# Projection banks of two token blocks, and a PSUM tile for scores alone

## Chip, cores and metric

The kernel runs on one core of a Trainium2 chip. The metric is device time of one execution in microseconds (us); the time before is the median of three runs. Four compute engines work from queues of their own, each in order: TensorE (PE, matmuls), VectorE (DVE), ScalarE (ACT) and GpSimd (POOL); SP issues the loads. Matmuls write to PSUM, which has eight banks of 512 fp32 values per partition; a bank goes to a new owner when its last reader has ended.

## What is computed

Two layers of an encoder on 512 tokens of width 1024, all fp32 in and out. Cut to what matters here:

```
h = rmsnorm(x, g_attn)
qa, ka, va, qb, kb, vb = split(h @ w_in)      # widths 512 128 128 512 512 512
qa, ka, qb, kb = rope(rmsnorm per head of 64) # each with a gain of its own
ya = windowed attention(qa, ka, va, sink)     # 8 query heads, 2 key heads, +/-128 tokens
yb = softmax(q1 k1) v - lam * softmax(q2 k2) v, normalised per head   # 4 heads
x = x + concat(ya, yb) @ w_out
h = rmsnorm(x, g_ffn); gate, val = split(h @ w_up)       # 2816 each
x = x + (silu(conv3(gate)) * val) @ w_down
```

## The kernel before

Activations stand transposed (features on partitions) as eight tiles of 128 x 512. To keep fp32 accuracy every operand is split into a high part and a low rest, and `mm3` makes each product of three matmuls. Weights come in units (`emit_unit`): one load, a cast on ACT (L193), a subtraction on DVE or POOL (L194).

`project` multiplies the four token blocks of 128 tokens by a chunk of 256 columns of `w_in`: 24 matmuls of 256 columns per block into one PSUM bank (half of it used), then a callback takes the bank. For queries and keys that is `qk_out`: ACT reads the bank and applies the row norm (`raw`, L343), ACT squares, DVE sums per head (`ss`) and scales (`sv`), POOL takes a power (`rs`, `rqa` or `rqb`, L255); for keys DVE multiplies by `rs` (L354); then rope: a product with the swapped halves (L360), a product with the cosine table (L364) and a sum (L365), the last two on POOL; then PE transposes the block into the single `tq` bank (`tr_qa`, `tr_bk` and so on, L369), and ACT and DVE split it into high and low (L258, L259). Values (`bv_done`) go from the bank through one instruction of ACT and one of DVE (L375, L376).

Attention runs as a generator, `attend`: first 8 steps of windowed attention (`a_scores`, `a_values`), then 16 of differential attention (`b_scores`, `b_weights`, `b_values`, `b_norm`). `a_scores` makes two score tiles of two banks (`sc_a`), whose masked maxima DVE takes (L429); ACT makes exponentials, DVE normalises the rows (`so_a`, L454), PE transposes them (`pt_a`, L470). `b_scores` makes one score tile of two banks (`sc_b`): a maximum on DVE (L518), a small product (L519), two exponentials on ACT (`e_b`, L522), a reciprocal (L526), the combination (L530); `b_weights` transposes it (`wt_b`, L542), `b_values` multiplies by values (`yb`), `b_norm` sums squares (`ss_yb`) and spreads factors over partitions (`rt_yb`).

`weave` writes these steps alternately with those of the projections and of the output projection (`wo`). A scheduler then orders each engine's instructions with a cost model of its own, and gives out buffers of pools by tag. What stands where in an engine's queue is thus fixed before the run. PSUM's tags: `mm` two banks, `at` two tiles of two banks (scores, some transposes, early projections), `acc` one, `tq` one. The channel mixer takes banks by `wide2`, in turn two `at` tiles and the pair of `mm`. SBUF: `rp` holds `raw` and the squares (7 tiles of one block), `tab` the rope tables (3), `sum` one norm sum.

Of the kernel before, what the change touches and what calls it, by code (L numbers as in the profile page):

```python
# [33 lines left out]
RP = 7  # L34
# [8 lines left out]
def kernel(  # L43
# [38 lines left out]
    def rp(name):  # L82
        return sb.tile([P, CW], F32, tag="rp", bufs=RP, name=name)

# [9 lines left out]
    def at2(name):  # L94
        return ps.tile([P, 2, S], F32, tag="at", bufs=2, name=name)
# [9 lines left out]
    def wide2(name):  # L105
        cyc["i"] += 1
        if cyc["i"] % 3 == 0:
            return mm(f"{name}a"), mm(f"{name}b")
        t = at2(name)
        return t[:, 0], t[:, 1]  # L110

    def halves(pick):
        have = []

        def alloc(name):
            if not have:
                have.extend(pick(name))
            return have.pop(0)
        return alloc

    def both(name):
        t = at2(name)
        return t[:, 0], t[:, 1]
# [130 lines left out]
    def rsqrt(o, i):  # L254
        nc.gpsimd.tensor_tensor(out=o, in0=i, in1=nhalf.broadcast_to([P, i.shape[1]]), op=ALU.pow)  # L255
# [23 lines left out]
    for l in range(depth):  # L279
# [43 lines left out]
        def project(name, done, alloc):  # L323
            w = [next_unit(), next_unit()]
            for t in range(NT):
                bank = alloc(f"pj{l}_{name}_{t}")
                for k in range(NK):
                    mm3(bank[:, :CW],
                        (h_in.hi[k][:, t * P:(t + 1) * P], h_in.lo[k][:, t * P:(t + 1) * P]),
                        (w[k // 4][0][:, k % 4, :], w[k // 4][1][:, k % 4, :]), k == 0, k == NK - 1)  # L330
                    if k % 4 == 3:
                        if k == NK - 1:
                            done(bank, t)
                        yield 1.3

        def qk_out(bank, t, n, tab, dst, nm, rq):
            nh = n // HD
            nm = f"{nm}{l}_{t}"
            if n == P:
                raw = bank  # L340
            else:
                raw = rp(f"raw_{nm}")
                nc.scalar.activation(raw, bank[:, :n], AF.Copy, scale=r_tok[:, t:t + 1])  # L343
            sq = rp(f"sq_{nm}")[:, :n]
            nc.scalar.activation(sq, raw, AF.Square)
            ss = smp(f"ss_{nm}", nh)
            nc.vector.tensor_reduce(out=ss, in_=sq.rearrange("p (h d) -> p h d", d=HD), axis=AX, op=ALU.add)
            sv = smp(f"sv_{nm}", nh)
            rv = raw.rearrange("p (h d) -> p h d", d=HD)
            if rq is None:  # L350
                nc.vector.tensor_scalar(out=sv, in0=ss, scalar1=1.0 / HD, scalar2=EPS, op0=ALU.mult, op1=ALU.add)
                rs = smp(f"rs_{nm}", nh)
                rsqrt(rs, sv)
                nc.vector.tensor_tensor(out=rv, in0=rv, in1=rs.unsqueeze(2).broadcast_to([P, nh, HD]), op=ALU.mult)  # L354
            else:
                nc.vector.tensor_scalar(out=sv, in0=ss, scalar1=EPS * HD, scalar2=None, op0=ALU.add)
                rsqrt(rq, sv)
            tb = sq
            sv_ = tab[:, 1, t].rearrange("p (two d) -> p two d", two=2).unsqueeze(1).broadcast_to([P, nh, 2, 32])
            (nc.vector if nm[1] == "a" else nc.gpsimd).tensor_tensor(out=tb.rearrange("p (h two d) -> p h two d", two=2, d=32),  # L360
                                    in0=raw.rearrange("p (h two d) -> p h two d", two=2, d=32)[:, :, ::-1, :],
                                    in1=sv_, op=ALU.mult)
            cv = tab[:, 0, t].unsqueeze(1).broadcast_to([P, nh, HD])
            nc.gpsimd.tensor_tensor(out=rv, in0=rv, in1=cv, op=ALU.mult)  # L364
            nc.gpsimd.tensor_tensor(out=raw, in0=raw, in1=tb, op=ALU.add)  # L365
            tr = tq(f"tr_{nm}")
            nb = n // P
            for b in range(nb):
                nc.tensor.transpose(tr[:, b * P:(b + 1) * P], raw[:, b * P:(b + 1) * P], ident)  # L369
            split_out(dst[0][:, :, t * P:(t + 1) * P] if nb > 1 else dst[0][:, t * P:(t + 1) * P],  # L370
                      dst[1][:, :, t * P:(t + 1) * P] if nb > 1 else dst[1][:, t * P:(t + 1) * P],
                      tr[:, :n].rearrange("p (b q) -> p b q", q=P) if nb > 1 else tr[:, :n])
# [11 lines left out]
        def akv_done(bank, t):  # L384
            raw = rp(f"raw_kv{l}_{t}")
            nc.scalar.activation(raw, bank[:, :CW], AF.Copy, scale=r_tok[:, t:t + 1])
            split_out(va[0][:, t * P:(t + 1) * P], va[1][:, t * P:(t + 1) * P], raw[:, P:])
            qk_out(raw[:, :P], t, P, tabs[1], ka, "ka", None)

        run(project("akv", akv_done, halves(both)))  # L390
# [4 lines left out]
        def proj_a(i, alloc):  # L395
            yield from project(f"aq{i}", lambda bank, t: qk_out(
# [94 lines left out]
        def bv_done(half, bank, t):  # L491
            if t % 2 == 0:
                v = keep(f"vb{l}_{half}_{t}")
                vb[half, t // 2] = (v[:, 0], v[:, 1])
# [316 lines left out]
```

## Time and profile before

| | |
|---|---|
| runs | 1347.71, 1350.54, 1353.40 us; median 1350.54 |
| profiled execution | 1350.17 us, span on the core 1348.4 us |
| busy: PE, DVE, ACT, POOL | 1256.2, 759.9, 550.7, 382.9 us |
| loads | 102.93 MB, 76 GB/s over the span |

The profiled execution is a run of its own. Its span goes from the first to the last instruction; the 1.8 us around it belong to the execution's time. "Idle before" and waits are put down to what ended them. PEclk is the clock granted to PE as a share of full speed: 0.50 is half. In rows of tiles the three numbers are shortest, median and longest duration in ns; in the timeline they are start and duration in us.

### The profile page before, as it was taken

What the parts mean: (1) busy time and instruction counts of PE and PEld (TensorE: products, weight loads), DVE (VectorE), ACT (ScalarE), POOL (GpSimd) and SP (SyncE); (2) the same over time, 40 slices, a digit from 0 to 9 for tenths busy, and PEclk for the clock granted to TensorE, in tenths of its full rate; (3) what the DMA queues carried; (4) which work ended last, traced back from release to release, by engine and by line L of the source; (5) the groups of instructions that cost most, each with busy time, mean ns of one, the idle gap of its engine ahead of it and who ended that gap; (6) DMA issues with size and microseconds to landing.
All of it is one profiled execution on the core that took longest, in us unless ns stands there. A gap on an engine that the chain in (4) does not pass through costs nothing.

```text
span 1348.4 us, 17285 instructions
## 1 busy us (share of the span) xinstructions
PE 1256.2 (93%) x6648; PEld 1048.1 (78%) x6648; DVE 759.9 (56%) x1345; ACT 550.7 (41%) x1003; POOL 382.9 (28%) x438
## 2 busy tenths in 40 slices
PE   6988799899999999999999688989999999999998
PEld 5977687687888778887788576967888887788876
DVE  6657687667555324554357676757755543355432
ACT  4445565445433212333345455634544331233321
POOL 5855377123211000110147461742221110011100
PEclk7998899699999999999999989989999999999999
DMA  4211122012332233332322020111133222333232
GB/s 167 82 44 32 40 63 63 16 47 79 95 101 90 82 101 94 98 100 69 98 91 63 32 63 8 57 63 32 48 99 104 94 87 90 106 94 97 83 102 78
DMA packets 32625, 102.93 MB, mean 76 GB/s; under 512 B 3616, under 2 KB 4000, under 8 KB 32544
## 3 DMA queue, kind: packets, MB, share of 16 engines
q1 hardware_dynamic: 32544, 101.84, 24.3%
q8 instruction: 52, 0.85, 0.3%
q14 instruction: 29, 0.24, 0.1%
HBM read 99.73 MB, written 2.10 MB: 76 GB/s over the span
## 4 chain that ended last, share of the span: by engine, by line
PE 75%; DVE 12%; ACT 5%; issue 4%; POOL 3%; DMA 1%; SPq 0%; POOLq 0%; ACTq 0%; DVEq 0%
PE up L207 8%; PE up L208 8%; PE up L206 8%; PE dn L207 4%; PE dn L206 4%; PE dn L208 4%; ACT so_a L447 2%; DVE so_a L454 2%; PE wo L206 1%; PE wo L207 1%; PE wo L208 1%; PE sc_b L516 1%; DVE so_a L429 1%; ACT wh L193 1%; PE wt_b L542 1%
## 5 line engine op out<-in xcount | busy, mean ns | idle before, releaser
L193 ACT CAST wh<-wr 128x1024 fp32r<-128x1024 f32 (+3 forms) x210 | 197.6, 945 | 401.4 <-PE up L207 151.7
L194 DVE TENSOR_TENSOR wl<-wr,wh 128x1024 fp32r<-128x1024 f32 (+3 forms) x174 | 191.7, 1105 | 170.0 <-ACT wh L193 165.0
L716 POOL TENSOR_TENSOR cv<-cv,rb 128x512 f32<-128x512 f32 x44 | 57.0, 1297 | 536.5 <-ACT cv L715 536.5
L207 PE MATMUL up<-nf_l,wh 128*128 128x512 f32 x464 | 180.9, 390 | 1.0 <-DVE nf_l L225 1.0
L206 PE MATMUL up<-nf_h,wh 128*128 128x512 f32 x464 | 180.6, 389 | 0.0
L208 PE MATMUL up<-nf_h,wl 128*128 128x512 f32 x464 | 180.5, 389 | 0.0
L194 POOL TENSOR_TENSOR wl<-wr,wh 128x1024 fp32r<-128x1024 f32 x36 | 86.7, 2413 | 99.4 <-ACT wh L193 85.7
L207 PEld LDWEIGHTS up<-nf_l,wh 128*128 128x128 f32 x464 | 87.1, 188 | 19.7 <-DVE nf_l L225 1.9
L206 PE MATMUL dn<-act,wh 128*128 128x512 f32 x240 | 96.1, 400 | 6.4 <-ACT wh L193 3.5
L206 PEld LDWEIGHTS up<-nf_h,wh 128*128 128x128 f32 x464 | 87.1, 188 | 18.1
L208 PEld LDWEIGHTS up<-nf_h,wl 128*128 128x128 f32 x464 | 87.1, 188 | 17.8
L207 PE MATMUL dn<-act,wh 128*128 128x512 f32 x240 | 95.9, 400 | 0.4 <-DVE act L259 0.4
L208 PE MATMUL dn<-act,wl 128*128 128x512 f32 x240 | 94.9, 398 | 0.0
L522 ACT ACTIVATE e_b<-sc_b,mx_b,rqb 128x512 f32<-128x512 f32 x64 | 49.3, 775 | 49.0 <-DVE mx_b L519 42.2
L709 DVE TENSOR_TENSOR gp<-up,rb 128x512 f32<-128x512 f32 x29 | 20.1, 692 | 80.6 <-PE up L208 79.6
L206 PEld LDWEIGHTS dn<-act,wh 128*128 128x128 f32 x240 | 45.4, 189 | 20.9 <-ACT wh L193 4.3
L715 ACT ACTIVATE cv<-cv 128x512 f32<-128x512 f32 x44 | 27.6, 632 | 79.7 <-DVE cv L714 79.6
L207 PEld LDWEIGHTS dn<-act,wh 128*128 128x128 f32 x240 | 45.8, 191 | 11.9 <-DVE act L259 1.1
L208 PEld LDWEIGHTS dn<-act,wl 128*128 128x128 f32 x240 | 45.4, 189 | 10.6
L206 PE MATMUL pj_bv<-wh,na_h 128*128 128x256 f32 x128 | 41.0, 320 | 7.7 <-DVE vb L376 7.7
L731 DVE TENSOR_TENSOR x<-x,dn 128x512 f32<-128x512 f32 x22 | 15.1, 688 | 52.8 <-PE dn L208 52.8
L470 PE MATMUL pt_a<-ident,so_a 128*128 128x128 f32 x160 | 28.3, 293 | 17.3 <-DVE so_a L454 12.0
(506 smaller groups left out, 3268.6 us busy)
## 6 DMA issues: line engine op xcount, KB each, us to landing
wr<-w_up SPq DMA_DIRECT2D x88, 512.0 KB, 3.6
wr<-w_in SPq DMA_DIRECT2D x36, 512.0 KB, 3.5
wr<-w_down SPq DMA_DIRECT2D x32, 384.0 KB, 3.1
wr<-w_down SPq DMA_DIRECT2D x32, 320.0 KB, 2.9
wr<-w_out SPq DMA_DIRECT2D x16, 512.0 KB, 3.7
x<-xT SPq DMA_DIRECT2D x8, 256.0 KB, 5.7
outT<-x SPq DMA_DIRECT2D x8, 256.0 KB, 2.0
rows<-row_par SPq DMA_DIRECT2D x2, 260.0 KB, 4.2
```

Of the source, the lines that this page charges most:

```text
L193: nc.scalar.copy(hi[:, o], raw[:, o])
L194: eng.tensor_tensor(out=lo[:, o], in0=raw[:, o], in1=hi[:, o], op=ALU.subtract)
L206: nc.tensor.matmul(acc, lhsT=a[0], rhs=b[0], start=start, stop=False)
L207: nc.tensor.matmul(acc, lhsT=a[0], rhs=b[1], start=False, stop=False)
L208: nc.tensor.matmul(acc, lhsT=a[1], rhs=b[0], start=False, stop=stop)
L447: nc.scalar.activation(so[i][:, :n], so[i][:, :n], AF.Exp, bias=ngm[:, i:i + 1], scale=rqa[:, qb, 2 * ip + i // 2, i % 2:i % 2 + 1], accum ...
L454: nc.vector.tensor_scalar(out=so[i][:, :n], in0=so[i][:, :n], scalar1=rl[:, i:i + 1], scalar2=None, op0=ALU.mult)
L470: nc.tensor.transpose(tr[:, o:o + P], so[2 * i + g][:, b * P:(b + 1) * P], ident)
L522: nc.scalar.activation(e[c], sc[c], AF.Exp, bias=mx[:, c:c + 1], scale=rq[:, c:c + 1], accum_out=lsum[:, c:c + 1])
L709: nc.vector.tensor_tensor(out=g[:, 1:S + 1], in0=acc[0], in1=rb, op=ALU.mult)
L715: nc.scalar.activation(cv, cv, AF.Silu)
L716: nc.gpsimd.tensor_tensor(out=cv, in0=cv, in1=rb, op=ALU.mult)
```

## The change

PSUM: a tag `sc` with one tile of two banks is for scores; `at` becomes two single banks, for transposes. A projection bank takes two token blocks side by side, and one callback handles both: ACT reads them one by one (the row norm differs), everything behind it works on both at once, and all transposes of the pair share the `tq` bank. The key's scaling by `rs` moves behind rope. All of windowed attention's transposes go to `at`. `wide` deals five banks in turn (two `mm`, two `at`, one half of `sc`). `rp` becomes four tiles of two blocks; the norm sum shares the ring of the tables.

```diff
-RP = 7
+RP = 4
     def rp(name):
-        return sb.tile([P, CW], F32, tag="rp", bufs=RP, name=name)
+        return sb.tile([P, 2, CW], F32, tag="rp", bufs=RP, name=name)
-    def at2(name):
-        return ps.tile([P, 2, S], F32, tag="at", bufs=2, name=name)
+    def at(name):
+        return ps.tile([P, S], F32, tag="at", bufs=2, name=name)
+
+    def sc2(name):
+        return ps.tile([P, 2, S], F32, tag="sc", bufs=1, name=name)
...
+    def wide(name):
+        cyc["i"] += 1
+        i = cyc["i"] % 5
+        return sc2(name)[:, 0] if i == 4 else (mm, at)[i % 2](name)
+
+    def turn(name):
+        cyc["i"] += 1
+        return (mm, at)[cyc["i"] % 2](name)
...
-            self.part = [sb.tile([P, S], F32, tag="sum", bufs=1, name=f"{name}_sum")]
+            self.part = [sb.tile([P, S], F32, tag="tab", bufs=3, name=f"{name}_sum")]
...
         def project(name, done, alloc):
             w = [next_unit(), next_unit()]
-            for t in range(NT):
-                bank = alloc(f"pj{l}_{name}_{t}")
...
+            for tp in range(NT // 2):
+                bank = alloc(f"pj{l}_{name}_{tp}").rearrange("p (t c) -> p t c", t=2)
+                for i in range(2):
+                    t = 2 * tp + i
+                    for k in range(NK):
+                        mm3(bank[:, i], (h_in.hi[k][:, t * P:(t + 1) * P], h_in.lo[k][:, t * P:(t + 1) * P]),
+                            (w[k // 4][0][:, k % 4, :], w[k // 4][1][:, k % 4, :]), k == 0, k == NK - 1)
+                        if k % 4 == 3:
+                            if i and k == NK - 1:
+                                done(bank, tp)
+                            yield 1.3
+
+        def scaled(name, bank, tp):
+            raw = rp(name)
+            for i in range(2):
+                nc.scalar.activation(raw[:, i], bank[:, i], AF.Copy, scale=r_tok[:, 2 * tp + i:2 * tp + i + 1])
+            return raw
+
+        def qk_out(raw, tp, tab, dst, nm, rq):
...
+            ss = smp(f"ss_{nm}", 2 * nh).rearrange("p (t h) -> p t h", t=2)
+            nc.vector.tensor_reduce(out=ss, in_=heads(sq), axis=AX, op=ALU.add)
...
-                nc.vector.tensor_tensor(out=rv, in0=rv, in1=rs.unsqueeze(2).broadcast_to([P, nh, HD]), op=ALU.mult)
...
+            for i in range(2):
+                sv_ = tab[:, 1, 2 * tp + i].rearrange("p (two d) -> p two d", two=2).unsqueeze(1).broadcast_to([P, nh, 2, 32])
+                (nc.vector if nm[1] == "a" else nc.gpsimd).tensor_tensor(
+                    out=tb[:, i].rearrange("p (h two d) -> p h two d", two=2, d=32),
+                    in0=raw[:, i].rearrange("p (h two d) -> p h two d", two=2, d=32)[:, :, ::-1, :],
+                    in1=sv_, op=ALU.mult)
+            cv = tab[:, 0, t2].unsqueeze(2).broadcast_to([P, 2, nh, HD])
+            nc.gpsimd.tensor_tensor(out=heads(raw), in0=heads(raw), in1=cv, op=ALU.mult)
             nc.gpsimd.tensor_tensor(out=raw, in0=raw, in1=tb, op=ALU.add)
-            tr = tq(f"tr_{nm}")
+            if rq is None:
+                nc.vector.tensor_tensor(out=heads(raw), in0=heads(raw), in1=rs.unsqueeze(3).broadcast_to([P, 2, nh, HD]),
+                                        op=ALU.mult)
             nb = n // P
+            tr = tq(f"tr_{nm}")[:, :nb * CW].rearrange("p (b q) -> p b q", b=nb)
             for b in range(nb):
-                nc.tensor.transpose(tr[:, b * P:(b + 1) * P], raw[:, b * P:(b + 1) * P], ident)
...
+                for i in range(2):
+                    nc.tensor.transpose(tr[:, b, i * P:(i + 1) * P], raw[:, i, b * P:(b + 1) * P], ident)
+            o = slice(tp * CW, (tp + 1) * CW)
+            split_out(dst[0][:, :, o], dst[1][:, :, o], tr)
...
-        run(project("akv", akv_done, halves(both)))
...
+        run(project("akv", akv_done, turn))
...
             for i in range(2):
-                sc = both(f"sc_{nm}_{i}")
+                scp = sc2(f"sc_{nm}_{i}")
+                sc = (scp[:, 0], scp[:, 1])
...
-                tr = mm(f"pt_{nm}_{b}") if b == 2 else both(f"pt_{nm}_{b}")[0] if b == 0 else tq(f"pt_{nm}_{b}")
+                tr = at(f"pt_{nm}_{b}")
...
+        def bv_done(half, bank, tp):
+            v = keep(f"vb{l}_{half}_{tp}")
+            vb[half, tp] = (v[:, 0], v[:, 1])
+            for i in range(2):
+                o = slice(i * CW, (i + 1) * CW)
+                v_out(bank[:, i], v[:, 0, o], v[:, 1, o], 2 * tp + i)
...
-            sc2 = at2(f"sc_{nm}")
-            sc = (sc2[:, 0], sc2[:, 1])
+            scp = sc2(f"sc_{nm}")
+            sc = (scp[:, 0], scp[:, 1])
...
-            tr = (mm(f"wt_b{l}_{h}_{qb}") if half and j else both(f"wt_b{l}_{h}_{qb}")[0])
+            tr = (mm if half and j else at)(f"wt_b{l}_{h}_{qb}")
...
             for f in range(f0, f1):
-                acc = wide2(f"up{l}_{f}")
+                acc = []
                 for j in range(2):
                     w = next_unit()
+                    a = wide(f"up{l}_{f}_{j}")
```

The changed code makes the scheduler write other queues. Two places on PE, both in layer 0. In the names, `sc_b0_2_1` is the differential score of layer 0, head 2, query block 1; `wt_b`, `yb`, `ss_yb` and `rt_yb` as above; the last number is only the tile's.

**Place 1**, the attention tail: the first scores of the second half of the heads. PE before:

```order
L369 MATMUL tr_bk10_2_2540<-ident_72,raw_bk10_2_2526 128x128 x2
L369 MATMUL tr_bk10_3_2617<-ident_72,raw_bk10_3_2603 128x128 x2
...
L516 MATMUL sc_b0_2_0_2630<-bkh0_1_1752,bql0_1_1751 128x512 x2
L516 MATMUL sc_b0_2_1_2677<-bkh0_1_1752,bqh0_1_1750 128x512 x2
...
L542 MATMUL wt_b0_1_3_2703<-ident_72,e_b0_1_3_0_2555 128x128 x4
L206 MATMUL yb0_0_1_2584<-wh_b0_1_2_2661,vb0_0_0_844 128x256
...
L516 MATMUL sc_b0_3_0_2735<-bkh0_1_1752,bqh0_1_1750 128x512 x2
```

and in the change:

```order
L516 MATMUL sc_b0_1_3_2331<-bkh0_0_706,bql0_0_705 128x512 x2
L542 MATMUL wt_b0_1_2_2451<-ident_72,e_b0_1_2_0_2234 128x128 x4
L580 MATMUL rt_yb0_0_0_2308<-ident_72,rr_yb0_0_0_2305 128x128 x4
L371 MATMUL tr_bk10_1_2403<-ident_72,raw_bk10_1_2387 128x128 x4
L516 MATMUL sc_b0_2_0_2418<-bkh0_1_1602,bqh0_1_1600 128x512 x2
...
L198 MATMUL yb0_0_1_2368<-wh_b0_1_2_2449,vb0_0_0_822 128x256
...
L516 MATMUL sc_b0_2_1_2465<-bkh0_1_1602,bqh0_1_1600 128x512 x2
...
L542 MATMUL wt_b0_2_0_2563<-ident_72,e_b0_2_0_0_2427 128x128 x4
L516 MATMUL sc_b0_3_0_2523<-bkh0_1_1602,bqh0_1_1600 128x512 x2
```

Two scores stood side by side before; now the 12 value matmuls `yb0_0_1` stand between them, one group `wt_b` before the third score, and the last score of the first half (`sc_b0_1_3`) has moved close ahead.

**Place 2**, the middle of windowed attention: the transposes of the first half's keys. PE before:

```order
L425 MATMUL sc_a0_1_2_0_1640<-ka0_213,qal0_1_416 128x384 x2
L369 MATMUL tr_bk00_0_1470<-ident_72,raw_bk00_0_1456 128x128 x2
L207 MATMUL pv_a0_0_3_1399<-p_a0_0_3_1_1438,va0_214 128x512
L208 MATMUL pv_a0_0_3_1399<-p_a0_0_3_1_1438,va0_214 128x512
L425 MATMUL sc_a0_1_2_1_1664<-ka0_213,qah0_1_415 128x384 x4
L425 MATMUL sc_a0_1_2_1_1664<-ka0_213,qal0_1_416 128x384 x2
L369 MATMUL tr_bk00_1_1544<-ident_72,raw_bk00_1_1530 128x128 x2
```

and in the change:

```order
L371 MATMUL tr_bk00_0_1408<-ident_72,raw_bk00_0_1392 128x128 x4
...
L200 MATMUL pj0_bv1_0_1616<-wh12_1001,na0_l0_120 128x256
L198 MATMUL pj0_bv1_0_1616<-wh12_1001,na0_h1_123 128x256
L425 MATMUL sc_a0_1_1_1_1369<-ka0_213,qah0_1_381 128x384 x4
L425 MATMUL sc_a0_1_1_1_1369<-ka0_213,qal0_1_382 128x384 x2
...
L371 MATMUL tr_bk00_1_1577<-ident_72,raw_bk00_1_1561 128x128 x4
```

Where two blocks' transposes stood four rows apart, a pair's four now stand in one row, the next pair's some 70 rows on, and two score tiles (`sc_a0_1_2_0`, `sc_a0_1_2_1`) that were neighbours stand apart with projection matmuls between.

More of the change, by code (lines that the diff above doesn't have):

```diff
@@ L358, in qk_out @@
+            rsqrt(rs, sv)
             tb = sq
[L359 to L363, printed above, removed]
@@ L395, in proj_a @@
         def proj_a(i, alloc):
[L396 to L397 removed]
+            yield from project(f"aq{i}", lambda bank, tp: qk_out(
+                scaled(f"raw_qa{i}{l}_{tp}", bank, tp), tp, tabs[0], qa[i], f"qa{i}",
+                rqa[:, 2 * tp:2 * tp + 2, 2 * i:2 * i + 2, :].rearrange("p t a b -> p t (a b)")), alloc)
         qk = {}
[L400 to L403 removed]
+        run(proj_a(0, turn))
+        run(proj_a(1, turn))
         y_hi = [None] * 8
```

93 lines of the change are left out of this document (24 added, 69 removed).

## Prediction

> **What bounds the kernel now.** I read the page first, then the table of stages, then TensorE's own waits, then its clock.
>
> ```profile
> span 1348.4 us, 17285 instructions
> ...
> PE 1256.2 (93%) x6648; PEld 1048.1 (78%) x6648; DVE 759.9 (56%) x1345; ACT 550.7 (41%) x1003; POOL 382.9 (28%) x438
> ...
> PE 75%; DVE 12%; ACT 5%; issue 4%; POOL 3%; DMA 1%; SPq 0%; POOLq 0%; ACTq 0%; DVEq 0%
> ```
>
> TensorE (PE) is busy 93% of the span and holds 75% of the chain that ended last. The change removes no matmul, so a gain can come only from PE's idle time (1348.4 - 1256.2 = 92.2 us) and from time at half clock. The table of stages tells where these are. The cuts are mine: 60.5 and 720 are where the first scores of a layer start, 213.7 and 873 where the last input projection has ended, 296.4 and 956 are close to the end of that layer's attention.
>
> ```profile
> core 0: us, PE busy (x) PEld busy (x) DVE busy (x) ACT busy (x) POOL busy (x), PEclk, DMA share, GB/s
> 60.50:213.70 153.20, 133.55 (x940) 116.63 (x939) 111.60 (x284) 85.59 (x213) 85.98 (x85) 0.93 0.15 44
> 213.70:296.40 82.70, 73.23 (x384) 57.93 (x384) 54.24 (x97) 36.86 (x75) 28.63 (x23) 0.88 0.15 45
> 296.40:690.00 393.60, 387.08 (x1765) 317.92 (x1764) 195.42 (x245) 139.79 (x182) 52.79 (x82) 1.00 0.30 93
> 720.00:873.00 153.00, 130.07 (x920) 112.37 (x920) 106.83 (x279) 84.96 (x213) 80.26 (x77) 0.96 0.14 42
> 873.00:956.00 83.00, 73.35 (x393) 57.02 (x392) 53.00 (x99) 36.89 (x74) 30.53 (x22) 0.90 0.14 45
> ```
>
> The channel mixer (296 to 690) leaves PE 6.5 us idle at full clock: nothing to win there. The two mixed stages (scores of attention woven with projections) leave 19.7 and 22.9 us, the two attention tails 9.5 and 9.7 us and a clock near 0.9. What PE waits for there:
>
> ```profile
> PE pt_a L470 <- DVE so_a L454: 12.0, 8, 2.0
> PE tr_bk L369 <- DVE bkl L259: 8.1, 6, 2.5
> PE pj_bv L206 <- DVE vb L376: 7.7, 4, 2.7
> ...
> PE pt_a L470 <- DVE bql L259: 5.3, 2, 3.8
> ...
> PE sc_b L516 <- DVE p_a L259: 2.2, 2, 1.9
> ...
> PE pj_bk L206 <- ACT raw_bq L343: 1.7, 1, 1.7
> ...
> PE pj_bq L206 <- ACT raw_bq L343: 1.2, 2, 0.6
> ...
> PE sc_b L516 <- DVE wl_b L259: 1.2, 3, 0.6
> ...
> PE sc_a L425 <- DVE p_a L259: 1.1, 1, 1.1
> PE pj_bq L206 <- DVE p_a L259: 0.9, 1, 0.9
> ```
>
> Columns: total us, times, longest. Except for the first row these are waits for a PSUM bank whose last reader is not done. The short ones cost twice, because the granted clock halves for a while after them. Six stretches of half clock in the mixed stages (from 117.0, 140.9, 158.0, 775.8, 803.1 and 816.8 us) each begin right behind such a bank wait; the first, the last and their sum:
>
> ```profile
> 117.00:120.40 3.40, 2.80 (x13) 2.80 (x14) 3.20 (x11) 1.07 (x2) 1.50 (x2) 0.50 0.49 154
> ...
> 816.80:820.20 3.40, 3.40 (x19) 3.40 (x18) 1.27 (x3) 0.00 (x0) 0.00 (x0) 0.50 0.00 0
> sum 23.90, PE 21.50 PEld 20.64 DVE 16.85 ACT 7.02 POOL 10.64; mean PE 3.58 PEld 3.44 DVE 2.81 ACT 1.17 POOL 1.77
> ```
>
> **The change part by part.**
>
> *Projection banks.* A bank now takes 48 matmuls before it is handed on, not 24, and two banks still alternate. Matmuls of 256 columns start 0.12 us apart at full clock:
>
> ```profile
> 195.91 0.28 PE L206 MATMUL yb<-wh_b,vb 128*128 128x256 f32 x1
> 196.03 0.28 PE L207 MATMUL yb<-wl_b,vb 128*128 128x256 f32 x1
> ```
>
> So the other bank is being filled for 48 x 0.12 = 5.8 us instead of 2.9 while this one is read. The 2.9 us added are more than the longest wait of this kind, 2.7, but the readers double as well, by one read of 256 columns on ACT and for values one on DVE, each about the 0.5 us of the windowed reduction quoted below. With 2.4 us of net slack, waits of 7.7 + 1.7 + 1.2 = 10.6 us in seven cases shrink to at most 0.3 in the two longest: I take all 10.6. If the readers came late by a whole further queue of work, half would stay: 5.
>
> *Chains on pairs.* The transposes of two blocks now go into one tq bank together and leave by one copy and one subtraction; tr_bk of the next block no longer stands right behind them (order, place 2). Windowed attention's transposes leave tq for the new single at banks. So 8.1 + 5.3 = 13.4 us of tq waits go; lower bound 8, if half of the tr_bk waits only move.
>
> *Scores apart from transposes.* Before, scores and transposed weights shared two double tiles. The waits of scores, and of one projection, for a transpose's reader go: 2.2 + 1.2 + 1.1 + 0.9 = 5.4 us.
>
> *Clock.* PE was busy 21.5 us in the six stretches at half speed; at full speed this is 10.75 us. The bounds are 0 and 10.75, and I take the upper, because each stretch begins behind a wait that is in the sums above. Gross: 10.6 + 13.4 + 5.4 + 10.75 = 40.1 us.
>
> The Trainium skill, "TensorE: Matmul & The Clock Gate", section "HAM oscillation — how this bites in real kernels", has the rule that PE needs idle gaps over some 3.4 us to fall back to the slow clock. By it only the one wait of 3.8 us would have cost clock, and the sum below would end near 1341 in place of 1334; the rows disagree with it, since five of the six stretches follow waits of 2.7 us at most.
>
> *One score tile instead of two: the price.* A score tile is busy from its matmuls until its last reader ends. For differential attention this is read off two rows of DVE (the reduction starts; the reciprocal starts when both exponentials are done) and two of PE (a score's first and last matmuls); then a group of four transposes; for windowed attention the readers are two masked reductions.
>
> ```profile
> 237.71 1.21 DVE L518 TENSOR_REDUCE mx_b<-sc_b 128x2 f32<-128x1024 f32 x1
> ...
> 240.88 0.16 DVE L526 RECIPROCAL rl_b<-bl 128x1 f32<-128x1 f32 x1 [1.76 <-ACT e_b L522]
> ...
> 260.33 0.50 PE L516 MATMUL sc_b<-bkh,bqh 64*128 64x512 f32 x2
> ...
> 260.89 0.40 PE L516 MATMUL sc_b<-bkh,bql 64*128 64x512 f32 x2
> ...
> 197.60 0.66 PE L542 MATMUL wt_b<-ident,e_b 128*128 128x128 f32 x4
> ...
> L429 DVE CUSTOM_DVE_ANT_0 so_a<-sc_a,mask_sb x64: 394/476/559, 62.0 to 822.4; 128x256 f32<-128x256 f32 x32, 128x384 f32<-128x384 f32 x32
> ```
>
> A differential score takes PE 260.89 + 0.40 - 260.33 = 1.0 us and holds the tile for 240.88 - 237.71 = 3.2 us more, a windowed one 2 x 0.5 and some 0.3 of starts and reads, 1.3 us. In the new order windowed scores stand at least 26 projection matmuls apart, 3.1 us: covered, unless DVE (73% busy: 111.6 of 153.2) comes to them late. I charge 0.15 us for each of the 32 tiles, 5 us; bounds 0 and 32 x 0.5 = 16, one DVE instruction of that length ahead of each.
>
> In the tail four differential scores per layer follow each other with little between (order, place 1). Cover between neighbours, in turn: three groups of four PE rows (wt_b, rt_yb, tr_bk; 3 x 0.7 = 2.1 us); 12 value matmuls (12 x 0.12 = 1.4); one group (0.7); two groups (1.4). Against 3.2 us this leaves 1.1 + 1.8 + 2.5 + 1.8 = 7.2 us a layer. The tails are idle 9.5 and 9.7 us today already, and what of that lies in this stretch then passes behind the longer wait. I take 5 us a layer, 10 in all; bounds 0 and 14.
>
> *Softmax distance.* Transposes of windowed attention wait 12.0 us for normalised rows, in 8 of 16 cases. In the new order they stand some 60 to 86 PE rows behind their last score, before mostly 73 to 130. If every case waited the longest, 2.0 us, it would be 32 us, 20 more; if shorter DVE queues made up for it, 0. I take 6, with one more half-clock stretch of 3.4 us a layer at half price each, 3.4: 9 us.
>
> *Less work on the other engines.* Pairing saves fixed parts. On POOL, one product of 512 costs 1.30 us against two of 256 at 0.74:
>
> ```profile
> L716 POOL TENSOR_TENSOR cv<-cv,rb x44: 1284/1296/1367, 337.8 to 1286.4; 128x512 f32<-128x512 f32 x44
> ...
> L364 POOL TENSOR_TENSOR raw_bq<-raw_bq,tab x16: 727/740/747, 94.7 to 866.8; 128x256 f32<-128x256 f32 x16
> ```
>
> That is 0.18 us for each of two products in 28 pairs, 10 us on POOL, and as an estimate the same on DVE and ACT, whose instruction counts halve in the same places. None of it is on PE's path, which sets the end, so I count 0: it lies beside matmuls. If that cover were gone, it would be worth up to 10 us of whichever engine then sets the end. The key's scaling after the rope instead of before it takes POOL's power out of the products' way: 0 by itself, its gain is in the tr_bk waits. The channel mixer's accumulators rotate over five banks, not six: each fills in 24 matmuls, far longer than the 1.3 us POOL product and its neighbours that free it; 0, and if the cover were gone it would show in a stage that idles 6.5 us today. Ring of rope buffers: four tiles of two blocks hold two chains, four blocks, where seven single tiles held three and a half: 0. Norm sums in the rope tables' ring put three POOL instructions of layer 1 (at most 1.3 us each) ahead of the norm factor that the first projection reads wait for: 0 to 4, taken as 0, because four banks, some 14 us of matmuls, stand between in the order. SP's weight loads keep their order; one small load of rows moves two places among them.
>
> **Sum.** 40.1 - 5 - 10 - 9 = 16 us. The profiled execution was 1350.17 with a span of 1348.4 and 1.8 around it; the runs' median is 1350.54, so the two agree. 1350.2 - 16 = 1334.
>
> **Rivals.**
> 1. *The score ring decides, slower.* One tile makes every score's matmuls wait for DVE, the engine with the second most work. Place: all 64 score tiles; the gain of 40 us is eaten when each adds 40.1 / 64 = 0.63 us. At 1.1 us, one reduction of 1.2 ahead in DVE's queue, it is 70 us: 1380. For it: DVE's load, and scores that DVE takes in strict order. Against: 3.1 us of cover in the mixed stages. Chance 0.15.
> 2. *The tail gives it back, no change.* The new order leaves 12 differential scores behind the last projection, before 9. If the three more run uncovered at 3.2 us plus 1 us of matmuls, that is 25 us for both layers, of which the earlier end of the projections returns half: 1334 + 13 = 1347. Chance 0.22.
> 3. *POOL holds DVE up.* The row below shows a two-column DVE instruction between 0.14 and 2.3 us: something holds it. Fused products hold 0.56 us longer; if each of 56 blocked a DVE instruction that PE waits for, 31 us, 1365; half of them, 1350. Chance 0.05. The Trainium skill, "SBUF — State Buffer", section "Who interferes with whom", says that a GpSimd instruction keeps a port pair shared with DVE for its whole length, which would be that something; no row here shows the port.
> 4. *More than the bank waits goes.* Shorter queues on DVE also end the 12.0 us of softmax waits and the ring costs nothing: 1350.2 - 40.1 = 1310. Chance 0.18.
>
> ```profile
> L519 DVE SCALAR_TENSOR_TENSOR mx_b<-mx_b,rqb x32: 143/160/2325, 172.9 to 944.1; 128x2 f32<-128x2 f32 x32
> ```
>
> **Numbers.** The forecast, 1326 to 1343 with 1334 as its value, has 0.40. About 0.5%, 7 us, is what a measurement of this kernel can tell from no change. Faster takes the forecast, rival 4 and a little of 3: 0.60; no change 0.22; slower 0.18. The range leaves out rival 1 and a little at the lower end: 1307 to 1358.
>
> **What would show it.** Right: no bank waits of pj_bv, pj_bq, pj_bk, tr_bk longer than 1 us; fewer half-clock stretches in the mixed stages; sc_b waiting for ACT's e_b four times a layer in the tail. Wrong: sc_a waiting for DVE's masked reductions in the mixed stages, so_a waits over 25 us, a tail longer than 90 us.

## The result, and the profile after

The changed kernel takes 1294.74 us (median of 4 runs, 1293.36 to 1296.44) against 1350.68 in the same comparison: a ratio of 0.9587, interval 0.9564 to 0.961. That is 56 us, where the forecast was 16. The profiled execution is 1294.65 us with a span of 1292.9. First lines of the page after:

```profile
span 1292.9 us, 17021 instructions
...
PE 1239.9 (96%) x6648; PEld 1040.6 (80%) x6648; DVE 754.8 (58%) x1245; ACT 541.8 (42%) x943; POOL 359.6 (28%) x354
```

PE's idle time fell from 92.2 to 1292.9 - 1239.9 = 53.0 us, 39 us less. The mean granted clock rose from 0.967 to 0.977; time lost to it is 1348.4 x 0.033 = 44.5 before and 1292.9 x 0.023 = 29.7 after, 15 us less. Together they make 54 of the 55.5 us by which the span is shorter.

The table of stages, cut in both kernels at the same events: first windowed score, end of the last projection, first matmul of the channel mixer, first of the next layer's projections. Before (the two mixed stages stand in the prediction with nearly the same cuts), then after:

```profile
0.00:60.60 60.60, 47.20 (x312) 44.63 (x312) 38.01 (x70) 26.75 (x56) 40.32 (x51) 0.89 0.39 128
...
213.90:306.20 92.30, 82.74 (x464) 67.24 (x463) 62.36 (x113) 40.83 (x81) 28.43 (x23) 0.89 0.15 46
306.20:682.40 376.20, 369.77 (x1621) 300.80 (x1620) 182.83 (x222) 131.97 (x172) 51.21 (x80) 1.00 0.30 93
682.40:720.00 37.60, 36.82 (x303) 36.11 (x301) 21.81 (x52) 17.75 (x37) 24.16 (x30) 1.00 0.27 84
...
875.30:970.50 95.20, 84.91 (x482) 67.92 (x482) 62.56 (x119) 40.72 (x80) 29.59 (x21) 0.91 0.14 45
970.50:1348.40 377.90, 368.74 (x1602) 299.95 (x1600) 171.51 (x209) 120.73 (x154) 40.64 (x73) 1.00 0.30 94
```

```profile
0.00:56.80 56.80, 45.17 (x327) 43.79 (x327) 33.92 (x53) 26.97 (x52) 32.68 (x39) 0.94 0.42 137
56.80:184.20 127.40, 120.40 (x881) 106.59 (x881) 98.45 (x233) 72.65 (x174) 70.83 (x49) 0.97 0.18 53
184.20:288.30 104.10, 90.64 (x525) 72.44 (x524) 74.55 (x134) 46.76 (x95) 31.02 (x20) 0.93 0.13 41
288.30:655.00 366.70, 366.27 (x1602) 299.28 (x1601) 185.44 (x219) 133.65 (x172) 56.23 (x86) 1.00 0.32 95
655.00:691.80 36.80, 36.80 (x309) 36.67 (x307) 20.11 (x39) 17.98 (x31) 23.46 (x22) 1.00 0.27 85
691.80:813.10 121.30, 119.29 (x894) 107.07 (x894) 91.66 (x229) 75.00 (x176) 74.04 (x51) 0.99 0.18 53
813.10:918.50 105.40, 91.23 (x491) 72.29 (x491) 72.10 (x128) 45.15 (x91) 26.66 (x17) 0.87 0.13 41
918.50:1292.90 374.40, 370.09 (x1632) 302.51 (x1630) 178.56 (x215) 123.62 (x157) 44.71 (x74) 1.00 0.31 95
```

The mixed stages are 153 and 155 us before, 127 and 121 after; their idle time fell from 19.7 and 22.9 to 7.0 and 2.0. The tails became longer, by 12 and 10 us, partly because they took over 61 and 9 matmuls, and idle 4 us more each; in the second layer's the clock is lower as well (0.87 for 0.91). The two mixer stages lost 13 us in length; their idle time fell from 6.4 and 9.2 to 0.4 and 4.3.

PE's own waits after (the four longest, then two that the prediction named):

```profile
PE sc_b L516 <- ACT e_b L522: 9.1, 10, 2.4
PE pt_a L470 <- DVE so_a L454: 7.3, 4, 2.2
PE wt_b L542 <- DVE e_b L530: 7.2, 5, 3.1
PE pj_akv L198 <- ACT wh L185: 6.2, 1, 6.2
...
PE tr_bk L371 <- DVE y_yb L582: 1.7, 2, 0.9
...
PE pt_a L470 <- DVE p_a L252: 1.2, 1, 1.2
```

The waits for a projection's bank and for the keys' reader of tq (`bkl`, `bql`) are gone; 1.7 us for another reader of tq (`y_yb`) and 1.2 us for the reader of an at bank (`p_a`) are left. Scores wait for the exponentials in the tail, four times in the first layer and six times in the second.

### The profile page after: what moved, and what is told of

It is laid out like the page before. It is cut to its first block, busy times and chain, and to the rows that moved or that the text cites. A ratio compares the mean times of both kernels' runs of the same rounds, so it can differ in the third digit from the quotient of the medians.

```text
span 1292.9 us, 17021 instructions
## 1 busy us (share of the span) xinstructions
PE 1239.9 (96%) x6648; PEld 1040.6 (80%) x6648; DVE 754.8 (58%) x1245; ACT 541.8 (42%) x943; POOL 359.6 (28%) x354
## 5 line engine op out<-in xcount | busy, mean ns | idle before, releaser
L199 PE MATMUL up<-nf_l,wh 128*128 128x512 f32 x704 | 274.7, 390 | 0.6 <-DVE nf_l L217 0.5
L200 PE MATMUL up<-nf_h,wl 128*128 128x512 f32 x704 | 274.1, 390 | 0.4
L198 PE MATMUL up<-nf_h,wh 128*128 128x512 f32 x704 | 273.4, 390 | 0.0
L199 PEld LDWEIGHTS up<-nf_l,wh 128*128 128x128 f32 x704 | 132.2, 188 | 29.8 <-DVE nf_l L217 2.8
L200 PEld LDWEIGHTS up<-nf_h,wl 128*128 128x128 f32 x704 | 132.2, 188 | 28.8 <-DVE wl L186 1.5
L198 PEld LDWEIGHTS up<-nf_h,wh 128*128 128x128 f32 x704 | 132.2, 188 | 27.5 <-ACT nf_h L216 0.2
L200 PE MATMUL dn<-act,wl 128*128 128x512 f32 x352 | 139.5, 397 | 0.0
L199 PE MATMUL dn<-act,wh 128*128 128x512 f32 x352 | 139.4, 397 | 0.0
L198 PE MATMUL dn<-act,wh 128*128 128x512 f32 x352 | 138.8, 395 | 0.0
L711 DVE TENSOR_TENSOR gp<-up,rb 128x512 f32<-128x512 f32 x44 | 30.3, 693 | 103.4 <-PE up L200 98.4
L199 PEld LDWEIGHTS dn<-act,wh 128*128 128x128 f32 x352 | 66.8, 190 | 16.5
L198 PEld LDWEIGHTS dn<-act,wh 128*128 128x128 f32 x352 | 66.0, 188 | 16.5
L518 DVE TENSOR_REDUCE mx_b<-sc_b 128x2 f32<-128x1024 f32 x32 | 39.0, 1219 | 7.9 <-PE sc_b L516 7.8
```

What stands on the lines that cost most here:

```text
L198: nc.tensor.matmul(acc, lhsT=a[0], rhs=b[0], start=start, stop=False)
L199: nc.tensor.matmul(acc, lhsT=a[0], rhs=b[1], start=False, stop=False)
L200: nc.tensor.matmul(acc, lhsT=a[1], rhs=b[0], start=False, stop=stop)
L518: nc.vector.tensor_reduce(out=mx, in_=scp, axis=AX, op=ALU.max)
L711: nc.vector.tensor_tensor(out=g[:, 1:S + 1], in0=acc[0], in1=rb, op=ALU.mult)
```

## Experiments

The theories: the pairs carry the gain (A), or the PSUM split does (B); within the split, the place of the windowed transposes, the score tile, or the mixer's banks. Each ratio is to runs of the kernel before in the same comparison, whose medians go from 1350.27 to 1352.67 us. The runs of e2 and e7 spread over 9 us each.

| run | what it is | median us | ratio to before, interval |
|---|---|---|---|
| e2 | after without the split | 1345.33 | 0.9955 (0.9933 to 0.9978) |
| e1 | before with the split | 1302.48 | 0.9629 (0.9608 to 0.965) |
| e3 | after, chains of one block | 1306.60 | 0.966 (0.9639 to 0.9681) |
| e4 | after, another order | 1300.60 | 0.9615 (0.9589 to 0.9641) |
| e5 | after, mixer banks in pairs | 1301.40 | 0.9649 (0.9634 to 0.9665) |
| e15 | after, keys scaled first | 1296.42 | 0.959 (0.9565 to 0.9614) |
| e6 | e1, transposes in at, tq, mm | 1334.34 | 0.9887 (0.9873 to 0.9902) |
| e9 | e1, transposes in at, at, mm | 1309.36 | 0.9683 (0.9658 to 0.9708) |
| e10 | e1, transposes in at, tq, at | 1313.38 | 0.9715 (0.9685 to 0.9745) |
| e7 | before, block 0 to mm | 1346.00 | 0.9963 (0.9946 to 0.998) |
| e11 | before, block 1 out of tq | 1333.43 | 0.9863 (0.9833 to 0.9892) |
| e13 | before, mixer banks one by one | 1341.42 | 0.9919 (0.9896 to 0.9942) |
| e14 | e13 with all three transposes in shared at | 1326.11 | 0.9799 (0.9772 to 0.9826) |
| e8 | after, score tile cut in two | 1300.48 | 0.9643 (0.9628 to 0.9658) |
| e12 | after, second place for tail scores | 1296.01 | 0.9584 (0.9553 to 0.9616) |

**e1, the split alone.** Three of its edits on the kernel before; at and sc2 are the change's, the mixer and the first projections take banks as there:

```diff
-                sc = both(f"sc_{nm}_{i}")
+                scp = sc2(f"sc_{nm}_{i}")
-                tr = mm(f"pt_{nm}_{b}") if b == 2 else both(f"pt_{nm}_{b}")[0] if b == 0 else tq(f"pt_{nm}_{b}")
+                tr = at(f"pt_{nm}_{b}")
-            tr = (mm(f"wt_b{l}_{h}_{qb}") if half and j else both(f"wt_b{l}_{h}_{qb}")[0])
+            tr = (mm if half and j else at)(f"wt_b{l}_{h}_{qb}")
```

> The kernel before, with only the PSUM split: one two-bank tile for scores, two single banks for transposes, banks dealt one by one in the channel mixer; projection banks and chains stay at one block. Theory A (the longer projection bank and the paired chains carry the gain, since bank waits and waits for the key's reader end with them): most bank waits of pj_bv, pj_bq, pj_bk and tr_bk stay, the mixed stages keep over 30 of their 42 us of idle time, 1325 to 1345 us. Theory B (scores that no longer share tiles with transposes carry it): mixed stages under 20 us idle, 1300 to 1315 us. Theory C (the score ring costs as my sum has it, and other things pay): over 1345 us.

**e2, the pairs alone**: the changed kernel with the split turned back, so for scores

```diff
-                scp = sc2(f"sc_{nm}_{i}")
-                sc = (scp[:, 0], scp[:, 1])
+                sc = both(f"sc_{nm}_{i}")
```

and likewise for the transposes, the mixer and the first projections.

> The changed kernel, with PSUM dealt as before: scores and transposes share two tiles of two banks, windowed attention's transposes go to three places, the channel mixer takes banks in pairs; projection banks of two blocks and their paired chains stay. Theory A (pairs carry the gain): 1300 to 1315 us, mixed stages under 20 us idle. Theory B (the split carries it): 1325 to 1345 us. Either theory: the tail's waits of scores for the exponentials, 9.1 us with the single tile, fall under 3 us, because two score tiles alternate again.

1302.48 and 1345.33: theory B. The split alone brings 49 us, the pairs alone 6. In e2 PE idles 1341.9 - 1248.7 = 93.2 us, 92.2 before, and the waits show where:

```profile
PE pt_a L477 <- DVE so_a L461: 19.4, 8, 4.2
...
PE pt_a L477 <- DVE mx_a L436: 5.3, 2, 2.7
...
PE sc_a L432 <- DVE p_a L260: 2.8, 2, 2.0
PE pj_bk L206 <- ACT raw_bq L341: 2.7, 2, 1.4
```

The bank waits for values are gone, as forecast, and windowed attention's transposes wait 19.4 us instead of 12.0: other waits took their place. A part of these has a cause of its own: two of the eight, 4.24 and 4.25 us, stand behind instructions of L461 that took 2.42 to 2.45 us beside POOL (last section).

**e3, banks of two blocks with chains of one** (`qk_one` is `qk_out` of the kernel before):

```diff
+        def qk_two(bank, tp, n, tab, dst, nm, rq):
+            for i in range(2):
+                t = 2 * tp + i
+                qk_one(bank[:, i], t, n, tab, dst, nm, None if rq is None else rq(t))
```

> The changed kernel, with banks of two blocks but chains of one block: norm, rope, transposes and split run for each block by itself behind the pair's last matmul, rp is seven tiles of one block again, the key is scaled before rope. Theory A1 (the longer bank is what counts): within 6 us of the changed kernel, 1290 to 1301. Theory A2 (fewer, larger instructions on DVE, ACT and POOL count, and one tq bank a pair): tr_bk and tr_bq wait 8 us or more again, 1310 to 1330 us.

1306.6: neither range but nearer to A2. Beside e1 (1302.5) the longer bank alone gains nothing, so what the pairs add to the split, 8 us, comes with the chains. The expected tr waits did not return, so e3 does not say which part of the chain it is.

**e4, order**:

```diff
-ATT = 92.0
+ATT = 93.0
```

> The changed kernel with one weight of the weaving 93 instead of 92: no work, no bank and no wait is changed by it, only the order in which steps are written. It shows how far the order alone moves the time. If the gain beyond my forecast is luck of the order, it moves by more than 10 us; if it belongs to the change, it stays within 6 us of 1294.7.

1300.6, 6 us slower for no change of work: it is one sample of what a new order alone does. So the 8 us between e1 and the changed kernel are little more than that, and the 49 are far above it.

**e5, mixer in pairs**, and **e13, mixer one by one** in the kernel before:

```diff
-                acc = wide2(f"up{l}_{f}")
+                acc = []
...
+                    a = wide(f"up{l}_{f}_{j}")
```

> The changed kernel, with the channel mixer's accumulators taken in pairs again: the pair of mm, the pair of at and the score tile in turn, six banks, where the change deals five one by one. Theory M (one by one a bank comes free as soon as its own reader is done, in pairs PE and the readers run in lumps): the 11 us of idle time that the change took out of the two mixer stages come back, most of it with dn waiting for ACT's casts, and the time is 1302 to 1309 us. Rival (the mixer gained because less work was left over from the stages before it): within 4 us of 1294.7.

> The kernel before, with one edit: the channel mixer takes its banks one by one, from mm and from the first halves of the at tiles in turn, four banks instead of six in pairs. Theory M (pairs make PE and the readers run in lumps): the mixer stages' idle time falls from 15.6 to under 7 us in both layers together, and the time to 1338 to 1346 us. Rival N (number of banks counts, or what the attention leaves behind): no gain, 1348 to 1360 us.

e13: 1341.4, 10 us faster, in theory M's range, though it has four banks in place of six. The mixer stages are 368.9 and 373.3 us long and idle 2.7 and 6.8: 9.5 us together for 15.6, not under 7 as I expected of M. e5: 1301.4, just under M's range and slower by 6.7, about the scale of e4; only 3.8 us of it are mixer idle time. My reading of the difference, not tested: in the kernel before two of three pairs are one tile and come free as a whole, in e5 two of three are two tiles. So dealing one by one is worth some 10 us in the kernel before.

**e6, e9, e10: where the windowed transposes go**, with everything else as in e1:

```diff
-                tr = at(f"pt_{nm}_{b}")
+                tr = (at, tq, mm)[b](f"pt_{nm}_{b}")
```

(e9 has mm for block 2 alone, e10 tq for block 1 alone.)

> The split-only kernel (1302.5 us), with the three transposes of a windowed unit at three places again: one in the single at banks, one in tq, one in the projection banks mm. Theory S (a score tile of its own is what counts): within 8 us of 1302.5. Theory P (where the transposes go is what counts, since they stand in the ring of the projections and of the keys' transposes): 1315 to 1335 us, bank waits of pj and tr back over 10 us.

> The split-only kernel (1302.5 us), with one of the three windowed transposes, block 2, in the projection banks mm; blocks 0 and 1 in at. Theory Q (tq is the knot: a windowed transpose in tq stands in turn behind the projections' transposes, 20 to 110 rows after its neighbour in PE's order of the kernel before, and the unit's values, its row buffers and the next maxima wait with it): 1298 to 1312 us. Theory P (mm is the knot: a projection's bank waits for a softmax): 1320 to 1340 us.

> The split-only kernel, with block 1 of the three windowed transposes in tq; blocks 0 and 2 in at. Theory Q: nearly all of the 32 us that the run with three places lost: 1322 to 1340 us. Theory P: 1298 to 1312 us.

Three places cost 32 us (1334.3), more than mm alone (7, about the scale of e4) and tq alone (11) together. Theory P for e6. e9 lies in Q's range, e10 1 us above P's and far below Q's, so neither theory holds for both. e6 loses its time in the mixed stages, which idle 19.8 and 15.7 us (e1: 7.7 and 8.4); `sc_a` waits 12.9 us for the maxima there, 3.6 in e1. Why both places together cost more than their sum was not settled.

**e7 and e11: one place changed in the kernel before.** e7 moves block 0 to mm; e11 is this one line:

```diff
-                tr = mm(f"pt_{nm}_{b}") if b == 2 else both(f"pt_{nm}_{b}")[0] if b == 0 else tq(f"pt_{nm}_{b}")
+                tr = mm(f"pt_{nm}_{b}") if b == 2 else both(f"pt_{nm}_{b}")[0]
```

> The kernel before, with one edit: the first transposes of each windowed unit go to the projection banks mm, not to a score tile, so that windowed scores share their two tiles with nothing else; all else as before. Theory S (scores and transposes block each other in the shared tiles): the time from the end of a unit's scores to its reciprocal, 13.6 us in the kernel before and 8 in the changed ones, falls under 10, and the time to 1320 to 1338 us. Theory P: no gain, 1345 to 1360 us, because more transposes now stand in the ring of the projections.

> The kernel before, with one word changed: block 1 of the windowed transposes goes to a shared score tile like block 0, not to tq; banks, chains, mixer and all else as before. Theory Q: waits of tr_bk for bkl and of pt_a for bql fall under 4 us, the time from scores to reciprocal under 11 us, and the time to 1315 to 1335 us, most of what the whole split brought. Theory S+Q (both tq and the shared score tile have to go): 1338 to 1352 us.

e7: 4 us, less than e4. Taking a transpose out of the score tiles gains nothing when it lands in the projections' banks. e11: 19 us from one line, in theory Q's range, though not most of the split's 49. The timeline shows the knot, in the third windowed unit of layer 0. In the kernel before, its scores are done at 80.83 + 0.34 = 81.2 us; DVE's first maximum starts at 94.5:

```profile
79.01 0.38 PE L369 MATMUL tr_qa<-ident,raw_qa 128*128 128x128 f32 x2
80.37 0.61 PE L425 MATMUL sc_a<-ka,qah 64*128 64x384 f32 x4
80.83 0.34 PE L425 MATMUL sc_a<-ka,qal 64*128 64x384 f32 x2
...
86.52 0.66 PE L369 MATMUL tr_qa<-ident,raw_qa 128*128 128x128 f32 x2
90.70 0.38 PE L369 MATMUL tr_qa<-ident,raw_qa 128*128 128x128 f32 x2
94.19 0.60 PE L470 MATMUL pt_a<-ident,so_a 128*128 128x128 f32 x4
...
94.50 0.56 DVE L429 CUSTOM_DVE_ANT_0 so_a<-sc_a,mask_sb 128x384 f32<-128x384 f32 x1 [1.33 <-PE pt_a L470]
```

The maximum writes its masked row to a buffer of `tmp`, of which there are eight, four a unit. They are held by the first unit, whose block 1 is to be transposed in tq, in turn behind four transposes of queries (`tr_qa`), each at the end of its own chain of norm and rope. That `pt_a` is the one at 94.19. The order places the maximum behind it, and even so DVE stands 1.33 us, with all that is queued behind it. In e11 the same transposes run right behind block 0, at 75.72, and the maximum of the unit's second tile starts 0.4 us behind its score:

```profile
75.72 0.60 PE L470 MATMUL pt_a<-ident,so_a 128*128 128x128 f32 x4
...
83.28 0.34 PE L425 MATMUL sc_a<-ka,qal 64*128 64x384 f32 x2
...
84.03 0.54 DVE L429 CUSTOM_DVE_ANT_0 so_a<-sc_a,mask_sb 128x384 f32<-128x384 f32 x1
```

Over the 16 units, from the end of the scores to the reciprocal (L452): 13.6 us before, 7.6 in e11, 8.1 in e1, 7.8 in the changed kernel, 15.3 in e7. The measure is not all that counts: it is 7.4 in e6, which is 32 us slower than e1.

**e14, all three transposes in the shared at tiles**, with e13's mixer:

```diff
-                tr = mm(f"pt_{nm}_{b}") if b == 2 else both(f"pt_{nm}_{b}")[0] if b == 0 else tq(f"pt_{nm}_{b}")
+                tr = both(f"pt_{nm}_{b}")[0]
```

> The kernel before, with that edit and with all three windowed transposes in the shared at tiles (none in tq or mm); scores still share the at tiles with them, projection banks and chains as before. Theory Q+M (place of the transposes and dealing are the whole of the split): within 8 us of the split-only kernel's 1302.5. Theory S (the score tile of its own adds to that): 1312 to 1330 us, with waits of sc_a, sc_b and pt_a for shared tiles over 10 us.

1326.1, theory S in time, but the waits for shared tiles that I expected are not there (`pt_a` for the maxima 2.5 us, `sc_b` for `wl_b` 2.9). What e1 has beyond it is 24 us: start stages of 53.2 and 36.4 us for 60.4 and 37.6 (8.4 us; their projections take banks one by one there), and 15 us in the mixed stages and tails, which would come from the score tile with the single at banks. These were not separated.

**e15, keys scaled first**: these lines stand ahead of rope again, not behind it:

```diff
+            if rq is None:
+                nc.vector.tensor_tensor(out=heads(raw), in0=heads(raw), in1=rs.unsqueeze(3).broadcast_to([P, 2, nh, HD]),
+                                        op=ALU.mult)
             tb = sq
```

> The changed kernel, with the keys scaled before rope as in the kernel before. My working costed this step at nothing: 1289 to 1300 us, within the 6 us that the order alone moves. Rival (POOL's power in front of the products holds the keys' transposes): 1301 to 1312 us, waits of tr_bk over 6 us.

1296.4, no difference: that step was costed at nothing and is nothing.

**e8, the score tile cut in two.**

```diff
-        return ps.tile([P, 2, S], F32, tag="sc", bufs=1, name=name)
+        return ps.tile([P, S], F32, tag="sc", bufs=2, name=name)
```

> The changed kernel, with the score tile cut into two tiles of one bank each: each half of a differential score has a maximum of its own and comes free behind its own exponential (32 more instructions on DVE). If the tail's waits of scores for the exponentials (9.1 us) are the price of one tile, they fall under 4 us and the time is 1284 to 1292 us. If the tail is bound by the chain of maximum, exponentials and combination on DVE and ACT, the wait only moves to wt_b (7.2 us now), and the time is 1292 to 1300 us.

The waits fell, `sc_b` for `e_b` to 6.7 us and not under 4, PE's idle time from 53.0 to 1298.5 - 1259.9 = 38.6 and the clock rose to 0.987; yet it is 6 us slower, just above both ranges. PE was busy 20 us longer at a faster clock. The page of e8:

```profile
span 1298.5 us, 17036 instructions
...
PE 1259.9 (97%) x6648; PEld 1051.7 (81%) x6648; DVE 750.3 (58%) x1277; ACT 542.1 (42%) x943; POOL 358.8 (28%) x354
```

A score's two halves use 64 rows of the array each. Side by side in PE's timeline of the changed kernel, then alone in that of e8:

```profile
209.69 0.50 PE L516 MATMUL sc_b<-bkh,bqh 64*128 64x512 f32 x2
210.03 0.39 PE L516 MATMUL sc_b<-bkl,bqh 64*128 64x512 f32 x2
210.26 0.40 PE L516 MATMUL sc_b<-bkh,bql 64*128 64x512 f32 x2
```

```profile
183.76 0.50 PE L514 MATMUL sc_b<-bkh,bqh 64*128 64x512 f32 x1
184.10 0.39 PE L514 MATMUL sc_b<-bkl,bqh 64*128 64x512 f32 x1
184.33 0.39 PE L514 MATMUL sc_b<-bkh,bql 64*128 64x512 f32 x1
```

Six matmuls take 210.26 + 0.40 - 209.69 = 0.97 us, three of one half alone 0.96. Cutting the tile let the order part the halves, and each then costs as much as both: of the 192 pairs of score matmuls 187 start within 40 ns of each other in the changed kernel, 79 in e8.

**e12, a second place for scores in the tail**, in the second half's odd heads:

```diff
+            two = half and j
+            scp = None if two else sc2(f"sc_{nm}")
+            sc = [at(f"sc_{nm}_{c}") for c in range(2)] if two else (scp[:, 0], scp[:, 1])
...
-            tr = (mm if half and j else at)(f"wt_b{l}_{h}_{qb}")
+            tr = (mm if half else at)(f"wt_b{l}_{h}_{qb}")
```

> The changed kernel, with a second place for scores in the tail: of the second half's differential heads every odd one takes the two at banks, halves side by side but maxima taken one by one (8 more instructions on DVE a layer), and its transposes go to mm. If the score ring costs what its waits show (sc_b for e_b 9.1 us, and the half clock behind it), 1280 to 1290 us. If the chain on DVE and ACT bounds the tail, or the order moves against it, 1290 to 1300 us.

1296.0, the same as the changed kernel. `sc_b` waits 16.0 us for `e_b` there, more than 9.1, and the tails idle 13.0 and 15.0 us, before the edit 13.5 and 14.2. So this second place gains nothing; whether the chain on DVE and ACT sets the tail's pace or the new order took the gain back is left open.

## Why the prediction was wrong

The direction was right and most named waits went, but the size was 40 us short, and the cause was put in the wrong part. By size the sum missed most at the softmax distance (9 us charged, 5 gained) and at the mixer (put at 0, 11 gained); by cause, at its first term. By the steps of the sum:

- **Projection banks and chains on pairs (24.0 us).** The waits went as forecast, but most of their gain was not the pairs': e2 has the pairs and gains 6. The step that failed is counting each wait as time that goes when its own cause goes. With the windowed transposes left in their three places, PE's idle time in e2 is what it was: the waits for `so_a` rose from 12.0 to 19.4 us, and 5.3 us of `pt_a` for the maxima are new. That all of them stood in one in-order loop, PE's transposes, DVE's maxima and tq, is my reading of it, and for a part of the 19.4 it does not hold.
- **The transposes leave tq.** I had the edit only as part of that 13.4. e11 gives 19 us for it alone. I read `pt_a` for `so_a`, 12.0 us, as softmax latency, and did not ask why DVE, 73% busy, began the maxima of a score tile on average 7.8 us after its last matmul.
- **Scores apart (5.4).** e1 against e14: 24 us, 8 of it in the start stages, which the sum left out.
- **Clock (10.75).** Measured 15 over the span, some 12 of it in the mixed stages, for which the term stood (153.3 x 0.07 + 155.3 x 0.04 = 16.9 before, 127.4 x 0.03 + 121.3 x 0.01 = 5.0 after). The six stretches behind bank waits went, as forecast. Three more, from 86.3, 103.4 and 745.1 us, stood behind waits for `so_a` and were not in my list; the changed kernel has three of that kind.
- **Score ring in the mixed stages (-5).** No wait of `sc_a` for DVE among the rows after; the price was nothing, since maxima now start 1.8 us behind their scores. With other places for the transposes it is not nothing, see e6. Rival 1 fell with it.
- **Tail ring (-10).** `sc_b` for `e_b` rose by 8.5 us, from 0.6. This term was about right; the second place of e12 did not bring it back.
- **Softmax distance (-9).** Wrong in sign: 12.0 became 7.3 us. I counted PE rows between score and transposes, when the unit's own latency was what fell, from 13.6 to 7.8. What is left of these waits has another cause, DVE held beside POOL (last section).
- **Mixer banks (0).** I weighed five banks against six and not how they come free. The stages idle 11 us less; in e13 that edit alone takes 6 us of idle time out of them and 10 us off the run. The 6.5 us of idle time that I took for the whole was one layer's; the other's was 9.2.

Correcting these: 16 + 5 + 14 for the distance + 11 for the mixer + 4 for the clock + 1.5 for the tail = 51.5 us; the start stages' idle time gives 2.6 more (13.4 + 0.8 to 11.6 + 0). That is about the 55.5 measured; it shows that the terms now agree with the waits and the clock, not which edit ended which wait. Rival 4, more goes than the bank waits, was the nearest, and was priced at the waits on the list alone; its conditions held in part, since 7.3 us of the softmax waits stayed and the tail's ring cost. Rival 3's mechanism, POOL holding DVE up, is in the rows of L454, though in the changed kernel beside POOL's weight subtractions, which both kernels have, and not beside the fused products. One of my signs of failure, a tail longer than 90 us, came true in a kernel that is 56 us faster (from the last projection to attention's last matmul 92.5 and 97.4 us, 82.9 and 83.0 before): a stage that takes over work from the one ahead of it may well be longer.

## What to carry to other kernels

A ring with one buffer joins all its users into one queue: before a latency-bound step shares a bank with another chain, look at what stands ahead of it in turn and which buffers it holds meanwhile. When an engine in the loop starts late though it isn't full, find the first instruction that it stands before; removing the waits further down may only put others in their place, as in e2. And give banks back one by one, unless, as with the two halves of a score, it is their being side by side that is fast.

## What the hardware showed

- **Half clock behind short waits.** The changed kernel has three stretches of 3.4 us at half clock left in its mixed stages, 0.6 to 2.0 us behind waits of 2.17, 1.98 and 2.01 us (PE's timeline, then windows; the third number from the end is the clock):

```profile
75.50 1.02 PE L470 MATMUL pt_a<-ident,so_a 128*128 128x128 f32 x6 [2.17 <-DVE so_a L454]
101.40 0.33 PE L470 MATMUL pt_a<-ident,so_a 128*128 128x128 f32 x1 [1.98 <-DVE so_a L454]
754.67 0.66 PE L470 MATMUL pt_a<-ident,so_a 128*128 128x128 f32 x4 [2.01 <-DVE so_a L454]
```

```profile
72.69:76.10 3.41, 1.10 (x9) 0.81 (x8) 3.41 (x5) 0.00 (x0) 2.34 (x1) 1.00 0.56 161
99.99:103.40 3.41, 1.73 (x11) 1.39 (x12) 3.41 (x8) 1.13 (x3) 1.92 (x3) 1.00 0.74 199
751.93:755.34 3.41, 1.40 (x14) 0.91 (x11) 3.41 (x6) 0.59 (x3) 2.27 (x1) 1.00 0.62 161
...
76.10:79.50 3.40, 3.40 (x18) 3.11 (x17) 3.33 (x11) 2.80 (x7) 0.00 (x0) 0.50 0.50 152
103.30:106.70 3.40, 3.40 (x19) 3.36 (x17) 3.34 (x9) 0.87 (x2) 3.29 (x4) 0.51 0.22 90
755.20:758.60 3.40, 3.40 (x19) 3.40 (x18) 3.37 (x11) 1.44 (x3) 1.97 (x3) 0.52 0.52 157
```

The clock changes on a grid of 3.41 us: the three stretches begin at 76.09, 103.40 and 755.34, 8 and 191 steps of 3.413 apart. In the steps just ahead of them PE idles 2.31, 1.68 and 2.01 us. In this kernel, from 30 us on, nine of the ten steps at full clock that idle 1.4 us or more are followed by half clock, and one of the 344 that idle less (in the kernel before 12 of 18, and one of 345). So in these traces it is the idle time within one step that goes with half clock, and several short waits in a step add up.

- **DVE held beside POOL.** Normalising a windowed row (L454) takes 0.41 us in the median and up to 2.64. In the changed kernel ten of the 64 take over 0.8 us. All ten run beside a weight subtraction on POOL (`wl`, 2.4 us) and end 0.15 to 0.22 us after one. All four waits of `pt_a` for `so_a`, 7.3 us, and with them the three stretches above, stand behind such instructions; in the kernel before it is four of the eight waits, 7.4 of 12.0 us. No run moved these subtractions, so this is read off the times and not tested.

```profile
L454 DVE TENSOR_SCALAR so_a<-so_a,rl_a x64: 336/411/2643, 70.5 to 785.9; 128x256 f32<-128x256 f32 x32, 128x384 f32<-128x384 f32 x32
...
749.82 5.06 DVE L454 TENSOR_SCALAR so_a<-so_a,rl_a 128x256 f32<-128x256 f32 x4
...
749.44 4.77 POOL L186 TENSOR_TENSOR wl<-wr,wh 128x1024 fp32r<-128x1024 f32 x2 [2.25 <-ACT wh L185]
```

- **Halves side by side are free.** 0.97 us for both halves of a score, 0.96 for one. The Trainium skill, "TensorEngine Tiling (Array Packing)", section "Overview", gives up to twice the speed for a contraction of at most 64 rows; these rows agree.
